# Nine loads of 1 to 15 rows behind the last store of a linear-attention kernel

## The chip, the cores and the metric

The kernel runs on one core of a Trainium2 chip. The metric is the device time of one execution in microseconds (us); lower is better. The engines of the core are named as in the profile: PE (TensorE, matrix products), PEld (its weight loads), DVE (VectorE), ACT (ScalarE), POOL (GpSimd) and SP (SyncE, which only issues DMAs and waits). Each engine runs its own instructions in order; DMAs are issued by an engine's sequencer (POOLq, SPq) and carried out by 16 DMA engines that all queues share.

## The reference

Inputs Q, K and V have the shape (8, 12, 512, 64) in float32: 96 heads of 512 rows of 64. For each head

```
Q_feat = max(0, Q) + 1
K_feat = max(0, K) + 1
KV     = K_feat^T V                 (64 x 64)
K_sum  = sum of K_feat over rows    (64)
out    = (Q_feat KV) / (Q_feat K_sum + 1e-10)
```

The three inputs and the output have 12.6 MB each; the kernel reads 37.75 MB and writes 12.58 MB.

## The kernel before

The 96 heads are worked through in 12 groups (g = 0 to 11) of eight heads. For each group the kernel loads K, V and Q, makes the features on DVE (line 137), lays V out in blocks of a larger tile on DVE and ACT (lines 155 and 153), multiplies K features by V on PE (line 171), transposes the Q features on PE (line 192), multiplies them by KV (line 205), and divides on DVE (lines 222 and 223) into the tile `o_sb`, which is stored to DRAM.

Loads and stores go through two queues. POOL issues all loads but one (lines 106 and 112; they cast to bf16 on the way) and the stores of groups 0 to 9 (line 126). SP issues four DMAs: the first half of the first K load at the beginning (line 93, tile `k_first`, 1 MB), and at the end the store of group 10 (line 129, 1 MB) and the store of group 11 in two halves (line 132, 512 KB each). Each of these three stores waits for the DVE instructions that write its part of `o_sb`.

The order on every engine is that of the program: the body stands under `tc.manual_schedule()`, so nothing is moved. The framework adds the semaphores. Every DMA gets a completion semaphore; an instruction that needs the data waits for it. In the trace's records POOL's DMAs carry the semaphores 101 to 108 in turn, and SP's four DMAs carry 109, 112, 113 and 114. After the body, at line 327, the framework's closing code has SP wait for every semaphore in use, two to an instruction, and then runs a barrier over all engines and clears the semaphores.

The change stands right behind the last stores, lines 300 and 301:

```
        for g in range(last - LAG, NG):
            store(g)
```

with `last` = 11, LAG = 3 and NG = 12, so that the loop stores the groups 8 and 9 (on POOL) and 10 and 11 (on SP).

Of the kernel before, what the change touches and what calls it, by code (L numbers as in the profile page):

```python
# [8 lines left out]
FP32 = mybir.dt.float32  # L9
# [10 lines left out]
def kernel(  # L20
# [19 lines left out]
    nc = tc.nc  # L40

    B, H, S, D = Q.shape
# [41 lines left out]
    bufs = {}  # L84
# [6 lines left out]
    def load_first_k():  # L91
        k_raw = head_pool.tile([P, 2, C2, D], FP32, name="k_first")
        nc.sync.dma_start(out=k_raw, in_=k_dram[:, 0:4:2])
        raw["k", 0] = k_raw

    def load(x, groups):
        s = groups[0] // 2
        if groups[0] % 2 == 0 or (x, s) not in bufs:
            bufs[x, s] = in_pool.tile([P, 4, C2, D], BF16, name=f"{x}_raw")
        if len(groups) == 2:  # L100
            ms = slice(0, 4)
            of = slice(4 * s, 4 * s + 4)
        else:
            ms = slice(groups[0] % 2, 4, 2)
            of = slice(4 * s + groups[0] % 2, 4 * s + 4, 2)
        nc.gpsimd.dma_start(out=bufs[x, s][:, ms], in_=drams[x][:, of])  # L106
        for g in groups:
            raw[x, g] = bufs[x, s][:, g % 2 : 4 : 2]

    def load_q(s):  # L110
        t = in_pool.tile([P, 2, C4, D], BF16, name="q_raw")
        nc.gpsimd.dma_start(out=t, in_=q_eights[:, 2 * s : 2 * s + 2])  # L112
        rows = t.rearrange("p n (r c) d -> p n r c d", c=C)
        for e in range(2):
            raw["q", 2 * s + e] = rows[:, :, :, 4 * e : 4 * e + 4]

    def load_pair(s):
        load("k", (2 * s, 2 * s + 1))
        load("v", (2 * s, 2 * s + 1))
        load_q(s)  # L120

    def store(g):
        s = g // 2
        o_to = o_dram[:, 2 * NP * s : 2 * NP * s + 2 * NP]
        if g < NG - 2:
            nc.gpsimd.dma_start(out=o_to[:, g % 2 : 2 * NP : 2], in_=outs[s][:, g % 2 : 2 * NP : 2])  # L126
            return
        if g == NG - 2:
            nc.sync.dma_start(out=o_to[:, 0 : 2 * NP : 2], in_=outs[s][:, 0 : 2 * NP : 2])
            return  # L130
        for h in range(2):
            nc.sync.dma_start(
                out=o_to[:, 2 * h + g % 2 : 2 * NP : NP], in_=outs[s][:, 2 * h + g % 2 : 2 * NP : NP]
            )
# [6 lines left out]
    def k_features(g):  # L141
        k_raw = raw.pop(("k", g))
        kf = kf_pool.tile([P, C2, 2, D], BF16, name="kf")
        for n in range(2):
            feature(kf[:, :, n], k_raw[:, n])
        kfs[g] = kf

    def v_blocks(g):
        v_raw = raw.pop(("v", g))
        for b in range(4):  # L150
            ps = slice(32 * b, 32 * b + 32)
            if b == 3:
                nc.scalar.copy(out=v_all[ps, g % 2, :, :, b * D : b * D + D], in_=v_raw[ps])  # L153
            else:
                nc.vector.tensor_copy(  # L155
                    out=v_all[ps, g % 2, :, :, b * D : b * D + D], in_=v_raw[ps]
                )

    def q_features(g):
        q_raw = raw.pop(("q", g))  # L160
        qf = qf_pool.tile([P, R, C // 2, 2, D], BF16, name="qf")
        for n in range(2):
            feature(qf[:, :, :, n], q_raw[:, n])
        qfs[g] = qf

    def keys_values(g):
        kf = kfs.pop(g)
        kva_ps = psum_kva.tile([P, 4 * D1], FP32, name="kva_ps")
        for c in range(C2):
            for n in range(2):  # L170
                nc.tensor.matmul(  # L171
                    kva_ps[64 * n : 64 * n + 64],
                    lhsT=kf[:, c, n, :],
                    rhs=v_all[:, g % 2, n, c, :],
                    start=(c == 0),
                    stop=(c == C2 - 1),
                )
        kva = kva_diag[g % NV]
        for n in range(2):
            ps = slice(64 * n, 64 * n + 64)  # L180
            nc.scalar.copy(out=kva[ps, :, n, 0:D], in_=kva_ps[ps, 0 : 4 * D].rearrange("p (b d) -> p b d", b=4))  # L181
            nc.scalar.copy(out=kva[ps, :, n, D], in_=kva_ps[ps, 4 * D : 4 * D1])  # L182

    def transposes(g):
        qf = qfs.pop(g)
        if g % 2 == 0:
            qts[g // 2] = mid_pool.tile([P, C, P, R], BF16, name="qt")
        for half in range(2):
            qt_ps = psum_qt.tile([P, 2, R, P], BF16, name="qt_ps")
            for c in range(2):  # L190
                for r in range(R):
                    nc.tensor.transpose(qt_ps[:, c, r], qf[:, r, 2 * half + c, :, :], identity)  # L192
            copy = nc.vector.tensor_copy if half and g == NG - 2 else nc.scalar.copy
            lo = g % 2 * 4 + 2 * half
            copy(out=qts[g // 2][:, lo : lo + 2], in_=qt_ps.rearrange("p c r q -> p c q r"))  # L195

    def out_matmuls(g, h):
        qt = qts[g // 2]
        kva = kva_diag[(g // 2 * 2 + h) % NV]
        ops = [psum.tile([P, 2, BANK], FP32, tag="ps", name="o_ps") for _ in range(2)]  # L200
        for c in range(C):
            for j in range(2):
                b = 2 * (g % 2) + j
                q = 16 * (4 * h + b)
                nc.tensor.matmul(  # L205
                    ops[c // 4][64 * j : 64 * j + 64, c // 2 % 2, (c % 2) * W : (c % 2) * W + W],
                    lhsT=qt[:, c, q : q + 16, :],
                    rhs=kva[:, b],
                    start=True,
                    stop=True,  # L210
                )
        cells_of[g, h] = ops
# [19 lines left out]
    def output(g):  # L232
        for h in range(2):
            out_matmuls(g, h)
            norms(g, h)

    def clear(i):
        t = v_all[:, i].rearrange("p n c x -> p (n c x)").bitcast(FP32)
        w = t.shape[1] * 5 // 8
        nc.vector.memset(t[:, 0:w], 0.0)  # L240
        nc.scalar.copy(out=t[:, w:], in_=zero.to_broadcast([P, t.shape[1] - w]))  # L241
        nc.vector.tensor_copy(
            out=v_all[:, i, :, :, 4 * D : 4 * D1].rearrange("p n c j -> p (n c) j"),
            in_=ones[:, None, :].to_broadcast([P, 2 * C2, 4]),
        )

    with tc.manual_schedule():
        nc.gpsimd.memset(zero, 0.0)
        load_first_k()
        load("v", (0,))  # L250
        load_q(0)
        load("k", (1,))
        load("v", (1,))
        nc.vector.memset(ones, 0.0)
        for b in range(4):
            nc.vector.memset(ones[32 * b : 32 * b + 32, b : b + 1], 1.0)
        clear(0)
        make_identity(nc, identity)
        for t in kva_diag:
            for b in range(4):  # L260
                nc.gpsimd.memset(t[:, b], 0.0)  # L261
        load_pair(1)
        clear(1)
        last = NG - 1
        for g in range(last - 1):
            if g % 2:
                transposes(g - 1)
            k_features(g)
            v_blocks(g)
            if g >= 2:  # L270
                output(g - 2)
            if g % 2:
                transposes(g)
            else:
                q_features(g)
                q_features(g + 1)
            keys_values(g)
            if g % 2 and g // 2 + 2 < NG // 2:
                load_pair(g // 2 + 2)
            if g >= LAG:  # L280
                store(g - LAG)
        k_features(last - 1)
        output(last - 3)
        out_matmuls(last - 2, 0)
        v_blocks(last - 1)
        k_features(last)
        v_blocks(last)
        keys_values(last - 1)
        store(last - 1 - LAG)
        q_features(last - 1)  # L290
        q_features(last)
        norms(last - 2, 0)
        transposes(last - 1)
        out_matmuls(last - 2, 1)
        norms(last - 2, 1)
        transposes(last)
        keys_values(last)
        output(last - 1)
        output(last)
        for g in range(last - LAG, NG):  # L300
            store(g)


# [28 lines left out]
```

## Time and profile before

| what | us |
|---|---|
| median of 2 runs (lowest, highest) | 127.02 (126.63, 127.41) |
| span of the profiled execution, first to last instruction | 125.0 |
| last DVE instruction ends (line 223) | 117.87 |
| issues of the three stores on SP | 114.54, 116.22, 117.90 |
| their landings | 121.56, 122.82, 124.07 |
| busy DVE, PE, ACT, POOL in the span | 89.1, 62.7, 59.6, 26.1 |

The profile is one execution; its own run time is not listed, only its span, which is 2.0 us shorter than the median of the runs. Times in the profile count from the first instruction. A row of the form "a <- b: total, times, longest" gives how long a waited for b. "Time to landing" of a DMA goes from its issue to the last increment of its semaphore. Instructions of SPq are not counted as busy; their durations are the time that the sequencer records for the issue.

### The profile page before, as it was taken

Reading aid. Unit: us, or ns where it says so; the run is one execution under the profiler, and the core shown is the slowest. Engines: PE = TensorE matmul, PEld = TensorE weight load, DVE = VectorE, ACT = ScalarE, POOL = GpSimd, SP = SyncE. Lnnn points to the kernel's source line nnn. Section 1 sums busy time; section 2 is a strip of 40 time slices with the busy share of each in tenths; the row PEclk is TensorE's granted clock in tenths of the full one; section 3 lists DMA queues with packets and bytes.
Section 4 is the critical chain, followed back from the end, with each engine's and each line's share of the span. In section 5 each row is a group of like instructions: output and inputs, shape, how many; then the busy total and the mean of one; then the engine's idle time right before and its main releaser. Section 6 shows DMA issues by size and latency. Waiting matters only on the chain.

```text
span 125.0 us, 2348 instructions
## 1 busy us (share of the span) xinstructions
PE 62.7 (50%) x960; PEld 51.3 (41%) x960; DVE 89.1 (71%) x190; ACT 59.6 (48%) x86; POOL 26.1 (21%) x52
## 2 busy tenths in 40 slices
PE   0004945200593837539684691079494457775300
PEld 0003735200482827428573491057393255663100
DVE  4895444206999899997999930799948699969700
ACT  7532289306029781956539462601992295450000
POOL 6991023000001630233302430302020200020000
PEclk9999999955589999995999679756999558997555
DMA  3999999999999999999999999999999999999992
GB/s 94 329 220 207 208 195 208 209 213 214 210 210 212 219 214 207 211 214 220 227 404 328 213 212 214 215 347 391 228 211 216 216 267 417 420 410 417 408 403 103
DMA packets 11803, 32.13 MB, mean 257 GB/s; under 512 B 528, under 2 KB 528, under 8 KB 11792
## 3 DMA queue, kind: packets, MB, share of 16 engines
q0 software_dynamic: 10448, 28.84, 97.2%
q1 hardware_dynamic: 1344, 3.15, 6.7%
q8 instruction: 7, 0.11, 0.3%
q14 instruction: 4, 0.03, 0.1%
HBM read 37.75 MB, written 12.58 MB: 403 GB/s over the span
## 4 chain that ended last, share of the span: by engine, by line
DMA 53%; DVE 23%; PE 8%; ACT 6%; issue 3%; POOL 2%; POOLq 0%
DMA v_raw<-in_V_dram 53%; DVE v_all L155 8%; DVE o_sb L223 8%; PE kva_ps L171 5%; ACT v_all L153 3%; DVE qf L137 2%; PE qt_ps L192 2%; DVE recip L222 2%; ACT qt L195 2%; DVE kf L137 1%; DVE qt L195 1%; ACT kva_all L181 1%; POOL v_raw L106 1%; POOL k_raw L106 1%; PE o_ps L205 1%
## 5 line engine op out<-in xcount | busy, mean ns | idle before, releaser
L205 PE MATMUL o_ps<-kva_all,qt 128*64 128x130 bf16 x384 | 20.5, 244 | 36.9 <-DVE recip L222 27.3
L171 PE MATMUL kva_ps<-v_all,kf 128*64 128x260 bf16 x384 | 30.1, 322 | 15.5 <-DVE v_all L155 15.3
L155 DVE COPY v_all<-v_raw 32x2048 bf16<-32x2048 bf16 x36 | 25.8, 717 | 13.5 <-DMA v_raw<-in_V_dram 13.1
L223 DVE TENSOR_TENSOR o_sb<-o_ps,recip 128x512 f32<-128x512 f32 x48 | 33.2, 692 | 1.7
L171 PEld LDWEIGHTS <-kf 128*64 128x64 bf16 x384 | 24.7, 131 | 18.8 <-DVE v_all L155 15.7
L205 PEld LDWEIGHTS <-qt 128*64 128x64 bf16 x384 | 14.3, 120 | 42.1 <-issue 27.3
L153 ACT COPY v_all<-v_raw 32x2048 bf16<-32x2048 bf16 x12 | 22.6, 1893 | 17.1 <-DMA v_raw<-in_V_dram 16.9
L195 ACT COPY qt<-qt_ps 128x1024 bf16<-128x1024 bf16 x23 | 22.2, 1015 | 6.7 <-PE qt_ps L192 6.4
L181 ACT CAST kva_all<-kva_ps 64x256 bf16<-64x256 f32 x24 | 8.9, 371 | 27.7 <-PE kva_ps L171 27.5
L126 POOL DMA_DIRECT2D out_dram<-o_sb x10 | 8.6, 863 | 35.9 <-DVE o_sb L223 27.5
L192 PE MATMUL qt_ps<-identity,qf 128*128 128x128 bf16 x192 | 14.9, 236 | 1.8 <-ACT qt L195 1.2
L192 PEld LDWEIGHTS <-qf 128*128 128x128 bf16 x192 | 12.5, 106 | 4.5 <-issue 2.5
L137 DVE TENSOR_SCALAR kf<-k_raw 128x1024 bf16<-128x1024 bf16 x22 | 8.5, 429 | 7.8 <-DMA k_raw<-in_K_dram 7.8
L106 POOL DMA_DIRECT2D k_raw<-in_K_dram x6 | 4.9, 811 | 35.2 <-DVE kf L137 35.2
L222 DVE RECIPROCAL recip<-o_ps 128x8 f32<-128x8 f32 x48 | 9.6, 200 | 1.4 <-PE o_ps L205 1.2
L137 DVE TENSOR_SCALAR qf<-q_raw 128x1024 bf16<-128x1024 bf16 x24 | 8.8, 432 | 2.1 <-DMA q_raw<-in_Q_dram 2.1
L106 POOL DMA_DIRECT2D v_raw<-in_V_dram x7 | 5.4, 766 | 13.1 <-ACT v_all L153 9.3
L240 DVE MEMSET v_all<- 128x2600 f32 x2 | 4.5, 2225 | 1.1 <-issue 1.1
L112 POOL DMA_DIRECT2D q_raw<-in_Q_dram x6 | 4.2, 708 | 0.0
L182 ACT CAST kva_all<-kva_ps 64x4 bf16<-64x4 f32 x24 | 4.1, 169 | 0.0
L241 ACT COPY v_all<-zero 128x1560 f32<-128x1560 f32 x2 | 2.9, 1488 | 0.0
L261 POOL MEMSET kva_all<- 128x130 bf16 x16 | 2.4, 201 | 0.0
(13 smaller groups left out, 5.7 us busy)
## 6 DMA issues: line engine op xcount, KB each, us to landing
out_dram<-o_sb POOLq DMA_DIRECT2D x10, 1024.0 KB, 25.9
q_raw<-in_Q_dram POOLq DMA_DIRECT2D x6, 1024.0 KB, 26.2
k_raw<-in_K_dram POOLq DMA_DIRECT2D x5, 1024.0 KB, 21.9
v_raw<-in_V_dram POOLq DMA_DIRECT2D x5, 1024.0 KB, 23.2
k_first<-in_K_dram SPq DMA_DIRECT2D x1, 1024.0 KB, 4.8
v_raw<-in_V_dram POOLq DMA_DIRECT2D x2, 512.0 KB, 10.7
out_dram<-o_sb SPq DMA_DIRECT2D x1, 1024.0 KB, 7.0
out_dram<-o_sb SPq DMA_DIRECT2D x2, 512.0 KB, 6.4
```

Source lines behind the costliest of these rows:

```text
L106: nc.gpsimd.dma_start(out=bufs[x, s][:, ms], in_=drams[x][:, of])
L126: nc.gpsimd.dma_start(out=o_to[:, g % 2 : 2 * NP : 2], in_=outs[s][:, g % 2 : 2 * NP : 2])
L137: nc.vector.tensor_scalar(out=dst, in0=src, scalar1=1.0, scalar2=1.0, op0=ALU.add, op1=ALU.max)
L153: nc.scalar.copy(out=v_all[ps, g % 2, :, :, b * D : b * D + D], in_=v_raw[ps])
L155: nc.vector.tensor_copy(out=v_all[ps, g % 2, :, :, b * D : b * D + D], in_=v_raw[ps])
L171: nc.tensor.matmul(kva_ps[64 * n : 64 * n + 64], lhsT=kf[:, c, n, :], rhs=v_all[:, g % 2, n, c, :], start=(c == 0), stop=(c == C2 - 1),)
L181: nc.scalar.copy(out=kva[ps, :, n, 0:D], in_=kva_ps[ps, 0 : 4 * D].rearrange("p (b d) -> p b d", b=4))
L192: nc.tensor.transpose(qt_ps[:, c, r], qf[:, r, 2 * half + c, :, :], identity)
L195: copy(out=qts[g // 2][:, lo : lo + 2], in_=qt_ps.rearrange("p c r q -> p c q r"))
L205: nc.tensor.matmul(ops[c // 4][64 * j : 64 * j + 64, c // 2 % 2, (c % 2) * W : (c % 2) * W + W], lhsT=qt[:, c, q : q + 16, :], rhs=kva[:, ...
L222: nc.vector.reciprocal(out=recip, in_=cells[:, :, :, :, D:D1])
L223: nc.vector.tensor_tensor(out=o_sb[:, 2 * h + g % 2 : 2 * NP : NP, 4 * i : 4 * i + 4].rearrange("p n (b c) d -> p b c n d", b=2), in0=cell ...
```

## The change

After the loop over the last stores, the kernel allocates nine tiles of 16 partitions by 128 float32 and loads into them the first 1, 2, 3, 5, 7, 9, 11, 13 and 15 rows of Q, seen as rows of 128 float32 (512 bytes). All nine loads are issued on SP. Nothing reads the tiles.

```
         for g in range(last - LAG, NG):
             store(g)
+        probe_pool = ctx.enter_context(tc.tile_pool(name="probe", bufs=1))
+        rows = Q.flatten_outer_dims().rearrange("(n two) d -> n (two d)", two=2)
+        for k in (1, 2, 3, 5, 7, 9, 11, 13, 15):
+            t = probe_pool.tile([16, 2 * D], FP32, name=f"probe{k}")
+            nc.sync.dma_start(out=t[0:k], in_=rows[0:k])
```

## The prediction

> **What bounds the kernel now.** I read the page's slices first, then the stretches at the end, then who the SP queue waits for. The page's second part shows the span in 40 slices:
>
> ```profile
> DVE  4895444206999899997999930799948699969700
> DMA  3999999999999999999999999999999999999992
> ```
>
> The DMA engines are busy in every slice: the body is bound by transfers, and nothing of the change runs there. The change sits behind the last store, so only the end matters. The table of stretches says for the end (its columns: the stretch, its length, busy time of PE, PEld, DVE, ACT and POOL, PE's clock, DMA share, GB/s):
>
> ```profile
> 114.50:117.90 3.40, 1.93 (x24) 1.20 (x24) 3.23 (x9) 0.00 (x0) 0.00 (x0) 0.50 1.03 411
> 117.90:121.00 3.10, 0.00 (x0) 0.00 (x0) 0.00 (x0) 0.00 (x0) 0.00 (x0) 0.50 1.05 406
> 121.00:124.10 3.10, 0.00 (x0) 0.00 (x0) 0.00 (x0) 0.00 (x0) 0.00 (x0) 0.50 0.54 209
> 124.10:125.00 0.90, 0.00 (x0) 0.00 (x0) 0.00 (x0) 0.00 (x0) 0.00 (x0) 0.50 0.00 0
> ```
>
> From 117.9 no engine computes; up to 124.1 the stores drain, and 0.9 us of closing work follows with no byte moving. Lines 129 and 132, the three stores on SP, answer so:
>
> ```profile
> L132 SPq DMA_DIRECT2D out_dram<-o_sb x2: 372/372/372, 116.2 to 117.9; - x2
> ...
> DMA to landing us min/median/max: 6.2/6.4/6.6
> ```
>
> The last issue is at 117.90, and 6.2 later (124.07 in the record) it has landed. The L129 store, issued at 114.54, lands 7.0 later (121.56), the first L132 store at 122.82. SP's waits name who waits for these landings, and the list of line 327's instructions, the closing code, says when:
>
> ```profile
> SPq L327 <- DMA out_dram<-o_sb: 5.4, 4, 2.0
> ```
>
> ```profile
> L327 SPq EVENT_SEMAPHORE  x10: 17/28/28, 119.3 to 124.9; - x10
> ...
> L327 SPq DRAIN  x3: 7/7/7, 124.2 to 124.5; - x3
> ```
>
> So the end is: last landing 124.07, the drain behind the last wait at 124.155, and 0.81 of barriers to 124.96. SP's first closing instruction starts at 119.28, 1.39 after the last issue. The single records stand 0.06 apart. There is slack on SP from 119.56 to 121.56 and no slack behind 124.07.
>
> **What the change adds.** Nothing is removed or moved. Nine loads, 66 rows of 512 bytes or 33.8 KB in all, go to tiles that nobody reads. Bytes are nothing: at the 406 GB/s of the row above they take 0.1 us. DVE, ACT, PE and POOL have no instruction in it. Each load costs an SP issue and, at the end, a landing that the closing code waits for.
>
> The term that matters is a wait that the diff does not write. A DMA reports its landing on a semaphore, and the records show eight of these for POOL, given in turn. A ninth DMA has to wait until the first user has landed. On POOL this is visible, in the timeline of 55 to 63 us and of 77 to 86:
>
> ```profile
> 59.41 1.13 POOL L126 DMA_DIRECT2D out_dram<-o_sb  x1 [1.93 <-DMA v_raw<-in_V_dram]
> ...
> 79.27 1.13 POOL L126 DMA_DIRECT2D out_dram<-o_sb  x1 [4.45 <-DMA v_raw<-in_V_dram]
> ```
>
> A store of o_sb has no use for v_raw; it waits because the v_raw load eight DMAs before it holds the same semaphore. SP has four DMAs now (line 93, line 129, line 132 twice), on four semaphores, so no row shows SP's ring; I take it to have eight as well. Then the loads of 1, 2, 3 and 5 rows take the four fresh ones; the load of 7 rows waits for the k_first load (landed at 5.6); 9 rows for the L129 store (121.56); 11 rows for the first L132 store (122.82); **13 rows for the last store (124.07)**; 15 rows for the load of one row. So two of nine loads can only be issued when the kernel used to be over.
>
> Their price, step by step:
>
> 1. Slot of one SP issue. The rows say 0.37 (L132), 0.38 (L129), 0.43 (L93) for the recorded part; the spacing cannot exceed the 1.39 from the last issue to the next SP instruction, which also holds whatever leaving the block costs. POOL's back-to-back issues stand 0.72 apart (2.14, 2.86, 3.57). I take 0.65, near POOL's and above SP's own record; the ends 0.37 and 1.39 stay for the range.
> 2. With 0.65 the first seven issues are at 118.55, 119.20, 119.85, 120.50, 121.15, 121.80 and 122.84. They hide under the draining stores, whose packets stand ahead of them in the same queue.
> 3. The load of 13 rows starts at 124.07 + 0.02 = 124.09, that of 15 rows at 124.74.
> 4. Landing of a small load. The slices of DMA traffic at the start show k_first's first bytes 1.1 after its issue; the last store's final packet ended at 123.73 and counted as landed 0.34 later. Lower end 1.44. Upper end: k_first's 4.8 less 1 MB at 408 GB/s (2.57), so 2.2. I take 1.8, the middle: landed at 126.54.
> 5. SP's walk. After the last issue SP needs the same 1.39 to its first closing instruction (126.13), and then ten waits in place of eight (four more semaphores, two to an instruction), 0.06 each: 0.62, so 126.75. That is just later than the landing with its last wait and drain (126.54 + 0.08 = 126.62).
> 6. End: 126.75 + 0.81 = 127.56, against 124.96: **+2.6 us**.
>
> The profiled span is 125.0, the median of the runs 127.02; the page doesn't give that execution's own run time, so I carry the 2.0 between them over unchanged: 129.6.
>
> Bounds: slot 0.37, landing 1.44 and no walk give 124.09 + 0.37 + 1.44 + 0.08 + 0.81 = 126.79, +1.8 (128.9). A slot above 0.77 makes the nine issues themselves late (117.90 + 8 x 0.77 = 124.06), and each 0.1 then costs 0.9: at 0.95 the last is issued at 126.45, and the end comes at 126.45 + 2.01 + 0.81 = 129.27, +4.3 (131.3). No gain is possible: no existing instruction waits less.
>
> Two rules beside these rows. The Trainium skill's "DMA: Bandwidth & Descriptors", section "Latency and other measured facts", puts the first byte of a DMA issued from SP at about 0.6 us, where this trace has 1.1. By the page the landing would come at 126.04 and the sum would not change, because SP's walk ends later; by it without the walk the end would be 0.5 earlier. The same page, section "Why a DMA increments its semaphore by 16 and not by 1", says that a DMA on fewer than 16 engines leaves the missing increments to the issuing sequencer. No row here shows that; it would lengthen just the slot, so it speaks for more than the records of the full-width transfers.
>
> **Rivals.**
>
> *No wait on a reused semaphore* (the other side: not slower). If SP had at least 13 semaphores, all nine issues would run from 117.90 on. With a slot of 0.4 the last is issued at 121.5, SP's walk ends at 123.5, and the loads land just behind the last store, say 0.2 later: 127.2. With 0.65 the last issue is at 123.75 and the walk ends at 125.76: +1.6, 128.6. It decides at the thirteenth DMA of the queue. Against it: the POOL rows. For it: SP's ring is not shown.
>
> *The SP issue is the bound.* If the 1.39 is all slot, the last load is issued at 117.90 + 9 x 1.39 = 130.41, and 1.39 + 0.62 + 0.81 later the kernel ends at 133.2: +8.3, 135.3. For it: the 1.39 has no other explanation in the trace. Against it: a recorded issue of 0.4. It takes over above 0.77.
>
> *The loads do not stand at the end.* They depend on nothing, so an order that put them ahead of line 129, whose issue waits 113.5 us, or that dropped them as unread, would leave 127.0. Against it: the order on SP is that of the program.
>
> **How the numbers follow.** The forecast as worked out has 0.78, its own range 128.9 to 131.3; the issue as the bound 0.08; no reuse wait 0.09; hidden or dropped 0.05. Two per cent, about what a measurement of this kernel can tell from no change, is 2.54 us or 129.56: the forecast stands on that line. Walk and landing give the same end by two separate ways, and the slot has more room above than below, so within the forecast I put 0.62 above the line. Slower: 0.78 x 0.62 + 0.08 = 0.56; same: 0.78 x 0.38 + 0.09 + 0.05 = 0.43; faster 0.01. The range goes from 128.4, which takes in the upper half of the no-reuse case, to 131.6, the 131.3 and the spread of the runs (0.4 to each side).
>
> **What would show it.** In the new profile SP's waits should list the diff's line waiting on out_dram<-o_sb, near 121.6, 122.8 and 124.1. Two issues of that line should come after 124.0, one slot apart, and the closing of line 327 should end some 0.8 after the later of walk and landing. Everything up to 117.9 should be unchanged. The prediction is wrong if the last issue of the new line is before 124, if the nine issues stand over 0.77 apart, or if a small load needs much more than 2.2 us.

## The result and the profile after

| kernel | median us | runs | lowest, highest |
|---|---|---|---|
| before | 127.02 | 2 | 126.63, 127.41 |
| with the nine loads | 128.81 | 2 | 128.72, 128.90 |

The ratio is 1.0156, interval [1.0114, 1.0197]: slower by 1.8 us, clear of the noise, but within two per cent. The profiled execution took 128.90 with a span of 127.1, 1.8 us apart. The slices of the page:

```profile
span 127.1 us, 2359 instructions
...
DVE  5894443207999999998999621999948799699100
DMA  4999999999999999999999999999999999999960
```

The body ends as it did (last DVE instruction at 117.91, before at 117.87); the DMA row has become weak in its last two slices of 3.2 us. The stretches of the end (length, busy time of PE, PEld, DVE, ACT and POOL, PE's clock, DMA share, GB/s):

```profile
118.00:121.00 3.00, 0.00 (x0) 0.00 (x0) 0.00 (x0) 0.00 (x0) 0.00 (x0) 0.50 1.06 411
121.00:124.10 3.10, 0.00 (x0) 0.00 (x0) 0.00 (x0) 0.00 (x0) 0.00 (x0) 0.50 0.56 212
124.10:125.00 0.90, 0.00 (x0) 0.00 (x0) 0.00 (x0) 0.00 (x0) 0.00 (x0) 0.50 0.00 1
125.00:126.10 1.10, 0.00 (x0) 0.00 (x0) 0.00 (x0) 0.00 (x0) 0.00 (x0) 0.50 0.05 13
126.10:127.10 1.00, 0.00 (x0) 0.00 (x0) 0.00 (x0) 0.00 (x0) 0.00 (x0) 0.50 0.00 0
```

Up to 124.1 the stores drain at the rates of before. Then comes what is new: 0.9 us in which next to nothing moves (1 GB/s), 1.1 us at 13 GB/s (the last two loads), and only then the closing microsecond. Whom the SP queue waits for (total, times, longest), and the instructions of the diff's line 306 and of the closing code, now line 332 (durations in ns, first and last start):

```profile
SPq L306 <- DMA out_dram<-o_sb: 3.0, 3, 1.1
...
SPq L332 <- DMA probe<-in_Q_dram: 0.8, 2, 0.5
```

```profile
L306 SPq DMA_DIRECT2D probe<-in_Q_dram x9: 273/306/653, 118.4 to 124.5; - x9
```

```profile
L332 SPq EVENT_SEMAPHORE  x12: 17/28/28, 124.9 to 127.0; - x12
...
L332 SPq DRAIN  x3: 7/7/7, 126.3 to 126.6; - x3
```

The first line is the wait that the diff does not write: three loads of Q wait for landings of stores of the output, 3.0 us in all, though they share no data with them. The last load is issued at 124.5, the closing begins at 124.9 and waits for the loads only. The single records complete it: the loads of 9, 11 and 13 rows wait on the semaphores 112, 113 and 114 of the three stores and start at 121.61, 122.90 and 124.14, 0.02 behind each landing. The load of 15 rows starts at 124.49 and has landed at 126.01; the drain behind the last closing wait starts at 126.27, where it was 124.16, and the end comes 0.83 later, at 127.10 (before 0.81).

### The profile page after: what moved, and what is told of

Read it like the earlier page. It is cut to its first block, busy times and chain, and to the rows that moved or that the text cites. A ratio compares the mean times of both kernels' runs of the same rounds, so it can differ in the third digit from the quotient of the medians.

```text
span 127.1 us, 2359 instructions
## 1 busy us (share of the span) xinstructions
PE 67.7 (53%) x960; PEld 55.0 (43%) x960; DVE 89.5 (70%) x190; ACT 59.6 (47%) x86; POOL 26.2 (21%) x52
## 4 chain that ended last, share of the span: by engine, by line
DMA 55%; DVE 19%; PE 8%; ACT 6%; issue 2%; POOL 2%; POOLq 0%
DMA v_raw<-in_V_dram 30%; DMA q_raw<-in_Q_dram 26%; DVE o_sb L223 8%; DVE v_all L155 5%; PE kva_ps L171 5%; ACT v_all L153 3%; DVE qf L137 2%; PE qt_ps L192 2%; DVE recip L222 2%; ACT qt L195 2%; POOL v_raw L106 1%; DVE qt L195 1%; ACT kva_all L181 1%; PE o_ps L205 1%; POOL k_raw L106 1%
## 5 line engine op out<-in xcount | busy, mean ns | idle before, releaser
L171 PE MATMUL kva_ps<-v_all,kf 128*64 128x260 bf16 x384 | 34.0, 350 | 15.9 <-DVE v_all L155 15.6
L171 PEld LDWEIGHTS <-kf 128*64 128x64 bf16 x384 | 27.0, 142 | 20.2 <-DVE v_all L155 15.9
L192 PE MATMUL qt_ps<-identity,qf 128*128 128x128 bf16 x192 | 16.6, 252 | 1.5 <-ACT qt L195 1.4
L192 PEld LDWEIGHTS <-qf 128*128 128x128 bf16 x192 | 14.0, 115 | 4.5 <-issue 3.1
```

The costliest lines, as they stand in the source:

```text
L171: nc.tensor.matmul(kva_ps[64 * n : 64 * n + 64], lhsT=kf[:, c, n, :], rhs=v_all[:, g % 2, n, c, :], start=(c == 0), stop=(c == C2 - 1),)
```

## The experiments

Three theories. A: the eighth and ninth load cost the time, because eight completion semaphores go round on SP and these two reuse those of the last store and of the first load. B: each load costs its share, 1.8 / 9 = 0.2 us. C: any load behind the last store adds a landing of its own, some 1.5 us.

Each run is set against runs of the kernel before taken with it, whose medians are 126.76 to 126.89. The ratio is an estimate over the runs, not the quotient of the two medians, and a difference in us is worked out from the ratio where nothing else is said.

**The changed kernel again.**

> The changed kernel again, for a tight interval on the same chip as the three beside it. All theories: 1.8 us over the kernel before, 128.8 us, ratio 1.014. The profile: the loads of 13 and 15 rows issued at 124.1 and 124.5, the last landing near 126.0, 1.5 us behind its issue.

Measured: 128.70 against 126.76, ratio 1.0144 [1.0116, 1.0173], 1.8 us. In this execution everything from line 129 on stands 0.7 us later; what follows the store's landing is the same: the loads of 13 and 15 rows are issued 0.35 apart (124.87 and 125.22), and the last lands 1.51 after its issue. In its waits too, three waits of line 306 for out_dram sum to 3.0.

**Five loads.**

```
-        for k in (1, 2, 3, 5, 7, 9, 11, 13, 15):
+        for k in (1, 2, 3, 5, 7):
```

> Only the loads of 1, 2, 3, 5 and 7 rows; none of them reuses the semaphore of a store. Theory A (the cost is the wait of the eighth and ninth load for the semaphores of the last store and of the first load): all five are issued by 120.3 and land with the last store, end within 0.2 us of the kernel before, 127.0 to 127.2. Theory B (each load costs its share of an issue, 1.8 / 9 = 0.2 us): 128.0. Theory C (any load behind the last store adds a landing of its own, 1.5 us): 128.5.

Measured: 127.26, ratio 1.0028 [1.0009, 1.0047]: 0.35 us. B asked for 1.0, C for 1.5. A is right in kind and 0.15 short. From the waits and the closing instructions of this run:

```profile
SPq L332 <- DMA probe<-in_Q_dram: 3.5, 1, 3.5
...
L306 SPq DMA_DIRECT2D probe<-in_Q_dram x5: 293/423/617, 118.7 to 120.8; - x5
...
L332 SPq DRAIN  x3: 7/7/7, 125.2 to 125.5; - x3
```

No wait of line 306 is left, and all issues are over by 121.1. But the closing waits stand in a fixed order by semaphore number, two to an instruction and 0.06 apart. The third names 109, which the load of 7 rows now holds until 124.74. It passes at 124.75, and seven more instructions come behind it, though their semaphores are already up: the drain starts 0.49 after the last store's landing (124.75), where it was 0.08 in the kernel before. The 0.41 more agree with the measured 0.35.

**Eight loads**, without that of 15 rows.

```
-        for k in (1, 2, 3, 5, 7, 9, 11, 13, 15):
+        for k in (1, 2, 3, 5, 7, 9, 11, 13):
```

> The load of 15 rows is left out; that of 13 rows still waits for the last store. Theory A: the last landing moves from 126.01 to 125.66, and one wait of 0.06 more stands behind it: 0.3 us less than the changed kernel, 128.5. B: 0.2 less, 128.6. C: 128.8, unchanged. With the run of five loads: A expects nearly all of the cost between the fifth and the eighth load, B three fifths of a microsecond.

Measured: 128.62, ratio 1.0141 [1.0104, 1.0178], 1.8 us. The intervals of eight and nine overlap, so the runs cannot tell the 0.3 us; the records can. From the landing of the load of 13 rows to the drain it takes 0.33 (125.56 to 125.89); with nine, from that load's landing to the drain, 0.61 (125.66 to 126.27). From five loads to eight the median rises by 1.36 us, most of the cost, where B has 0.6. That falls to A.

**The nine loads ahead of the stores.**

```
+        (pool, rows and the nine loads as in the change)
         for g in range(last - LAG, NG):
             store(g)
-        (pool, rows and the nine loads)
```

> The same nine loads, issued on SP ahead of the store loop, right behind the first load of K. SP then issues the three stores as its eleventh to thirteenth DMA, on semaphores whose earlier users landed long before. A and C: hidden, 127.0 us, within 0.2 of the kernel before; the page shows the stores issued at 114.5, 116.2 and 117.9 as before. B, taken as a cost of the issues wherever they stand: 128.8.

Measured: 127.17, ratio 1.0021 [1.0002, 1.004]: 0.27 us instead of 1.8, so the issues by themselves are not the cost. SP's waits:

```profile
SPq L332 <- DMA out_dram<-o_sb: 5.5, 4, 2.2
SPq L304 <- DMA k_first<-in_K_dram: 2.3, 1, 2.3
```

The reuse wait is there (line 304, for the k_first load), but at the beginning, where SP has 108 us to spare. Here too the closing waits run on behind the last store's semaphore: the wait passes at 124.21, three more follow, and the drain starts at 124.46, 0.27 after the landing, against 0.08. That is 0.18 of the 0.27.

**Only the loads of 13 and 15 rows.**

```
-        for k in (1, 2, 3, 5, 7, 9, 11, 13, 15):
+        for k in (13, 15):
```

> Only the loads of 13 and 15 rows, the same two that end the changed kernel, now the fifth and sixth DMA of SP on fresh semaphores. Theory A (reuse wait): issued at 118.4 and 118.8, landed with the last store near 124.1, 127.0 to 127.2 us. Theory B (a share for each load): 127.4. Theory C (any load behind the last store adds a landing): 128.5.

Measured: 126.93, ratio 0.9999 [0.9974, 1.0023]. SP's waits hold no line 306:

```profile
SPq L332 <- DMA out_dram<-o_sb: 3.8, 3, 1.4
```

The same two loads that carry the cost in the changed kernel cost nothing that can be measured as fifth and sixth DMA of the queue, at most 0.3 us by the interval. The load of 15 rows landed at 124.61, 0.16 behind the last store. C falls, and B's 127.4 lies outside the interval too.

**Nine loads of 16 rows.**

```
-        for k in (1, 2, 3, 5, 7, 9, 11, 13, 15):
+        for i, k in enumerate((16,) * 9):
```

> Nine loads of 16 rows each in place of 1 to 15: as many DMAs, the same waits for semaphores. Theory A: 128.8 us as the changed kernel, since only the count of DMAs matters. Rival D (the odd row counts are dear, because a DMA on fewer than 16 engines leaves increments of the semaphore to the sequencer): issues shorter by 0.05 to 0.1 us and the end some 0.1 to 0.3 earlier, 128.5 to 128.7.

Measured: 129.06, ratio 1.0145 [1.0104, 1.0186], as nine odd loads. D falls: the issue of the last load takes 0.42 recorded, longer than 0.37 for 15 rows, and it lands 1.64 after its issue, not sooner than 1.52. (In the same place of the order, eighth, 13 and 16 rows take 0.31 each.)

**The nine loads in reverse order.**

```
-        for k in (1, 2, 3, 5, 7, 9, 11, 13, 15):
+        for k in (15, 13, 11, 9, 7, 5, 3, 2, 1):
```

> The same nine loads in the reverse order, 15 rows first, 1 row last. The loads of 2 rows and 1 row now wait for the last store. If the 0.65 us that the issue of the 2-row load took in the changed kernel belongs to 2 rows, it now stands on the path: slot 0.70 in place of 0.35, 129.1 to 129.2 us. If it belongs to the place (second behind the last store), the second load, of 13 rows, takes 0.65 there, and the end stays at 128.7 to 128.8.

Measured: 128.43, ratio 1.0104 [1.0055, 1.0153]. Neither number was right: it tends to be cheaper than the changed kernel (the intervals overlap). The record, of the slowest of the four executions, says why:

```profile
L306 SPq DMA_DIRECT2D probe<-in_Q_dram x9: 231/293/717, 118.9 to 125.0; - x9
...
L332 SPq DRAIN  x3: 7/7/7, 126.4 to 126.7; - x3
```

The shortest issue, 231 ns, is now that of 2 rows on the path; 1 row took 252, and the two stand 0.28 apart. One row landed 1.19 after its issue, against 1.52 for 15 rows. From the last store's landing to the end it is 2.57, where the changed kernel has 2.98. The long issue (717 ns) does not belong to 2 rows: here it is the second load, of 13 rows, again off the path. It isn't bound to the second place either: when the changed kernel was run again, it was the third load (745 ns, 3 rows).

**Seventeen loads.**

```
-        for k in (1, 2, 3, 5, 7, 9, 11, 13, 15):
+        for i, k in enumerate((1, 2, 3, 5, 7, 9, 11, 13) + (15,) * 9):
```

> Eight more loads of 15 rows behind the nine. Theory A: the loads up to the twelfth DMA wait as before; the rest go at 0.41 us a slot (0.37 recorded and 0.04 between), so the last is issued at 124.5 + 8 x 0.41 = 127.8, lands 1.5 later, and the end is 3.3 us behind the changed kernel: 132.1. If the semaphores' second round binds (the twentieth DMA waits for the load of 13 rows, landed at 125.7), it does not show, since the slots come later. Theory B: 8 x 0.2 = 1.6, 130.4.

Measured: 132.40, ratio 1.0421 [1.037, 1.0472].

```profile
L306 SPq DMA_DIRECT2D probe<-in_Q_dram x17: 273/400/639, 119.0 to 128.6; - x17
```

The ninth load is issued at 125.09, the seventeenth at 128.62: 0.44 a slot, 3.5 in all, where 3.3 was expected. The records show the semaphores in the order 115, 116, 117, 118, 109, 112, 113, 114 and 115 again: a ring of eight. Behind the store's landing each further load costs its slot; ahead of it, little (0.35 us for five loads, nothing measurable for two).

**Four loads ahead, five behind.**

```
+        (the loads of 1, 2, 3 and 5 rows)
         for g in range(last - LAG, NG):
             store(g)
-        for k in (1, 2, 3, 5, 7, 9, 11, 13, 15):
+        for k in (7, 9, 11, 13, 15):
```

> The same nine loads on SP, 1 to 5 rows ahead of the store loop and 7 to 15 rows behind it: as many DMAs on the queue, five of them still behind the last store, but every semaphore that they reuse was freed long before. Theory A (reuse wait): no issue after 121.5, the loads land with the last store, and what is left is the row of closing waits behind the late first semaphore, eight or nine of 0.06 us: 0.3 to 0.5 us over the kernel before, 127.1 to 127.3. Theory B (0.2 us for each load behind): 1.0 us more. Theory C (a landing for any load behind): 1.5 us more.

Measured: 127.48, ratio 1.0049 [1.003, 1.0068]: 0.62 us, just above what A gave. All nine loads are there and five are behind the last store, among them those of 9 to 15 rows; only the semaphores that they reuse are free. SP's waits have none of line 309, that of the five loads, and its last issue starts at 120.7:

```profile
SPq L335 <- DMA probe<-in_Q_dram: 2.8, 1, 2.8
...
L309 SPq DMA_DIRECT2D probe<-in_Q_dram x5: 308/367/862, 118.6 to 120.7; - x5
```

So 1.2 us of the 1.8 are gone. The run changes two things, though: it also takes four loads from behind the store. What these four cost there by themselves was not run; if it is as much as all five loads cost in the run of five, 0.35 us, then 0.8 to 0.9 us are left for the reuse wait (an estimate). The remaining 0.62: queued behind the stores, the five loads land 0.18 to 0.20 apart, the last at 124.73, 0.41 behind the last store (124.33), and three closing waits follow, so that the drain starts 0.67 after that store, where it was 0.08. So loads that queue behind a store do cost a share, as B has it, but 0.6 us and not 1.0.

**The nine loads on POOL.**

```
-            nc.sync.dma_start(out=t[0:k], in_=rows[0:k])
+            nc.gpsimd.dma_start(out=t[0:k], in_=rows[0:k])
```

> The same nine loads at the same place of the program, but issued on POOL, whose eight semaphores are held by its own earlier DMAs, the last of which lands at 119.3. Theory A: the eighth load waits until 119.3, all land before the last store, and SP's closing has as many waits as before, so the time is that of the kernel before within 0.1 us; this also tells the 0.2 us that the run with the loads ahead still cost: if it is the four more closing waits it is gone here, if it is the loads' own traffic it stays. Theories B and C, if they are about the place in the program: 128.5 to 128.8.

Measured: 128.68, ratio 1.0141 [1.0113, 1.017]: 1.8 us, and A's number was wrong. The timeline of POOL, and the closing instructions:

```profile
114.29 0.50 POOL L306 DMA_DIRECT2D probe<-in_Q_dram  x1 [0.84 <-DMA out_dram<-o_sb]
116.77 0.51 POOL L306 DMA_DIRECT2D probe<-in_Q_dram  x1 [1.98 <-DMA out_dram<-o_sb]
119.39 0.98 POOL L306 DMA_DIRECT2D probe<-in_Q_dram  x2 [2.11 <-DMA out_dram<-o_sb]
```

```profile
L332 POOLq DRAIN  x3: 51/106/6333, 119.8 to 126.6; - x3
...
L332 SPq DRAIN  x3: 7/7/7, 125.0 to 126.4; - x3
```

The reuse waits come as A has them, up to 119.39. What A left out is what follows. The last load, issued at 119.88, landed only at 124.54, beside the stores of SP. And POOL's drain, which begins the closing barrier, lasted until 126.13 (119.80 + 6.33), 1.6 us after that landing. SP stood ready at 125.05 and waited. In the kernel before, POOL's drain ended at 120.50, 1.2 after POOL's last landing (119.27), 3.6 ahead of the last store's landing; the change of queue used that up. That the drain waits for these landings is read from the times of the two runs; no record names what it waits for. That the total equals the changed kernel's is a coincidence of two different waits. Whether the 0.27 us of the run with the loads ahead are all closing waits stays open.

**One load of 66 rows.**

```
-        for k in (1, 2, 3, 5, 7, 9, 11, 13, 15):
-            t = probe_pool.tile([16, 2 * D], FP32, name=f"probe{k}")
+        for k in (66,):
+            t = probe_pool.tile([66, 2 * D], FP32, name=f"probe{k}")
```

> One load of 66 rows behind the last store on SP, as many bytes as the nine in one DMA (the first 66 rows, not the first few nine times). Theory A: on a fresh semaphore, issued at 118.4, it lands with the last store or 0.2 us later: 126.8 to 127.0, 0 to 0.2 us over the kernel before. Theory C: 1.5 us over it.

Measured: 127.00 against 126.87, ratio 1.0001 [0.998, 1.0022]. The same number of bytes at the same place in one DMA costs nothing that can be measured. It loads 66 different rows, in place of the first few nine times.

```profile
SPq L332 <- DMA out_dram<-o_sb: 4.8, 4, 2.1
```

The closing code waits for stores alone; the load landed at 123.83, before the last store (124.22). C falls a second time.

## Why the prediction was right, and which terms were off

The mechanism is the one on record, and the runs show it: the loads of line 306 wait for the stores' semaphores, the same two loads cost nothing measurable on fresh ones, and where every reused semaphore was free (and four of the loads stood ahead of the stores) 1.2 us of the 1.8 were gone.

The number owes something to luck. The predicted 129.6 was 0.8 too high, and the measured 128.81 lies just below the lower end of the forecast's own range, 128.9. It is in the stated range because that began at 128.4 for the sake of the rival without a reuse wait (of whose 127.2 to 128.6 that is only the last 0.2, not the upper half). Some 0.26 of the 0.8 is not in the steps at all: the prediction carried over 2.0 us between span and run time. In every run that lists both, the kernel before included, it is 1.7 or 1.8. With 1.8 the same steps give 129.4, and the forecast's own range 128.6 to 131.1. Step by step:

- Step 1, the slot, was taken as 0.65 from POOL's spacing. On the path it was 0.35 (124.14 to 124.49), the recorded 0.31 and 0.04 between. SP's own row, 0.37 to 0.43, was the near one.
- Step 2, seven issues under the stores: right. The first five were over by 120.5, the sixth and seventh started at 121.61 and 122.90.
- Step 3, the load of 13 rows at 124.09: measured 124.14, with the store's landing itself 0.05 later.
- Step 4, the landing, taken as 1.8: measured 1.52, close to its lower end of 1.44. The 1.1 to the first byte, which went into it and was set against 0.6, counts from the start of the issue. From the end of the recorded issue the first packet came 0.64 later for k_first and 0.61 later for the loads of 13 and 15 rows, so the two figures need not differ.
- Step 5, SP's walk, failed. It read the 1.39 from the last issue to the first closing instruction as SP's own time. With the loads it was 0.42 (124.49 to 124.91). The 1.39 was a wait: the first closing instruction waits on the semaphore 105 of POOL's last store, which landed at 119.27, and the instruction stands at 119.28. The line "SPq L327 <- DMA out_dram<-o_sb: 5.4, 4, 2.0" had said so: four waits, and SP has only three stores. The walk thus did not set the end; the landing did. That walk and landing gave the same end was no support.
- What remains of the walk was not foreseen: the semaphores 116, 117 and 118 are asked after 115, so that three instructions, 0.19 us, run behind the last landing, beside the wait and drain that the sum had. The end came 1.10 behind the last landing, where the prediction's sign had some 0.8.
- Step 6: from the last store's landing to the end it is 2.98 in the changed profile (124.12 to 127.10) and 0.89 before, 2.09 more, where the sum had 2.6. Slot 0.30, landing 0.28 and walk, 0.13 over the landing path, are 0.71 too much, the 0.19 of the closing too little: 2.08. The 2.09 is of two single executions; the runs give 1.8.
- The chances put 0.56 on slower by over two per cent; it was 1.56 per cent, on the side that had 0.43. Steps 1, 4 and 5 and the carried 2.0 all erred upwards, so the line was not as near as it seemed.

The rival of the issue as the bound rested on the same misread 1.39. With nine loads, the five free issues stand 0.32 to 0.70 apart, under the 0.77 that it needed. The seventeen loads show where it begins: behind the landing, at 0.44 a load. The rival without a reuse wait is refuted by the three waits of line 306, and that of hidden loads by their place at the end.

On the increments, the row is that the semaphore of the 15-row load got 16 events, one at 125.02 and fifteen from 125.83 to 126.01, while in the run with 16 rows each load has 16 events and none ahead of its data. The Trainium skill's "DMA: Bandwidth & Descriptors", section "Why a DMA increments its semaphore by 16 and not by 1", says the sequencer writes the missing ones at once: the trace agrees, as far as one event ahead of the data shows it (who wrote it is not recorded). That this lengthens the issue, as the prediction feared, does not show: as ninth load, 1 row took 0.25, 15 rows 0.37 and 16 rows 0.42.

## What to carry to other kernels

Count the DMAs of a queue at its end: with a ring of eight semaphores, as here, the ninth DMA waits for the first to land, whatever its data, and behind the last store such a wait is followed by an issue and a full landing in the open. Put late small transfers ahead of the stores (0.27 us here in place of 1.8), or into one DMA (nothing measurable). Before a gap is booked as an engine's own time, ask which semaphore its next instruction waits for, and count the waits of a line against the transfers that it is said to wait for.

## What the runs showed that was not expected

- The closing waits run in order of semaphore number, 0.06 us each. A late landing on a low number is followed by all the higher ones: 0.41 us in the run with five loads.
- Small loads queued on SP behind a store land some 0.17 to 0.20 apart (five loads: 124.22, 124.39, 124.57, 124.74), some seven times the 27 ns that a packet of 512 bytes took.
- The landing of a small load once the stores are done grows with its rows: 1.19 us for one, 1.21 for two, 1.52 for 13 and 15, 1.64 for 16. Between 15 and 16 rows that is no difference: in the run of seventeen a load of 15 rows took 1.63.
- POOL's drain ended 1.2 us (kernel before) and 1.6 us (loads on POOL) after the last landing of a DMA issued there.
- One or two issues on SP took 0.5 to 1.0 us instead of 0.2 to 0.4, whatever their rows, always among the first three loads behind the last store and over by about 120.6. They were never on the path, and their cause stays open.
